# Combine weights by slot in one pass between gather products, and the last expert pair's weight splits moved back

## The chip, the cores and the metric

One core of a Trainium2 chip. The metric is the device time of one execution in microseconds (us); the kernel before takes 785.08 us, the median of three runs.

## The reference

`x` (256 tokens of 1024 features) passes a first block of two layers (sliding-window attention and a gated recurrence) and then a second block, whose last part is the one that matters here: a hierarchical mixture of experts and a gated projection.

```
g_val, g_idx = top_k(softmax(ht @ w_rg + b_rg), 1)          # one of 4 groups
e_val, e_idx = top_k(softmax(e_logits of that group), 2)     # two of its 4 experts
combine = sum(one_hot(g_idx * 4 + e_idx) * gate)             # tokens x 16
a, u = ht @ w_gate[e], ht @ w_up[e]                          # 1024 -> 256
hid = silu(a) * u * combine
x = x + sum over e of hid @ w_down[e]                        # 256 -> 1024
h3 = rms_norm(x, ple_norm_g)
x = x + sigmoid(h3 @ w_pg) * (p @ w_ple)
```

## The kernel before

Everything is in fp32. For the dense matrices a weight `w` is split into `whi` (a cast on ScalarE, ACT; L287) and `wlo = raw - whi` (on VectorE, DVE; L288), and three fp32r matmuls (L380 to L382) stand for one; the `raw` they are split from is streamed from `w_all` by SyncE (SP). The experts' weights are streamed by the same queue (L231), but used unsplit.

The expert stage goes as follows. Routing gives each token a place among the 64 slots of each of its two experts, and `D` (L1347; `slots[t]`, for `t` the first and second 128 tokens) is the 128 x 1024 matrix of ones and zeros that says which token stands in which slot; `NP` = 8 pairs of experts have 128 slots each. `gather(i, k, t, j)` (L1409) multiplies by `D` to bring the hidden rows (`hh`, `hl`) into slots, 512 slots at a time (`i` = 0, 1), for each of the eight blocks `k` of features; the four products over `t` and `j` sum up in one PSUM tile, copied to `hs`. `gate_up(q, j)` (L1460) multiplies the slots of pair `q` by half (`j`) of its gate and up weights. `product` forms the gated product `hid` on ACT (L1468) and DVE (L1469), where `cs` (the combine weight of each slot) comes in. `turn` transposes it to `hidT` (L1475, L1477), `down` gives `y` (L1488), split into `yh` and `yl` (L555), and `scatter` (L1503) brings it back to the tokens through `DT`, the transpose of `D` (`turn_slots`, L1430).

`to_slots` holds what needs doing once: counts of tokens by expert (`psp`, L1436, to `cnt` and `cnti`), `cs` from `psc` (L1442: for each pair `q` the product of `D` with the two columns of `comb` that belong to it, over both `t`), and `turn_slots(1)`. If any expert has more than 64 tokens, `overflow` (L1546) does the rest after a branch on `cnti`; otherwise each engine jumps over it. SP has its part in that branch.

The order on each engine is set by the Tile scheduler from the code's order, from `ahead` (a priority) and from `issue_after`. Weights are requested by `Stream.give`, a list of buffer kinds (`t4`: two transfers of 512 KB; `raw` and `t8`: one of 1 MB), and by `refill`, which gives again what a step has used up; a transfer waits on SP until its buffer's last reader is done, and those behind it on SP wait too. Once the last expert's weights are requested, `refill` goes on to the final projection's (`pg`) and prepares up to `cap` of its splits ahead, behind `st.after(*last)`, the split of `y` of the pair at hand; `cap` is set in `down` for the last three pairs:

```
        if q > NP - 4:
            g.st.after(*last)
            g.st.cap = (2, 4, 6)[q - NP + 3]
        g.st.refill()
```

Then `ple_out` does the rest: the last scatter and the addition to `x` (`finish`, L1512), `xw = x * wb` (L1612), transposes (`tr`, L1615), the split into `h3h` and `h3l`, and the products by `pg` (L380 to L382).

Of the kernel before, what the change touches and what calls it, by code (L numbers as in the profile page):

```python
# [9 lines left out]
F32 = mybir.dt.float32  # L10
F32R = mybir.dt.float32r
I32 = mybir.dt.int32
AF = mybir.ActivationFunctionType
OP = mybir.AluOpType
AX = mybir.AxisListType
# [10 lines left out]
NE = NG * EG  # L26
NP = NE // 2
# [581 lines left out]
def load_row(g, tag, src, n=DM):  # L609
    t = g.p.tile([128, n], F32, tag=tag, name=tag, bufs=g.nwb if tag == "wb" else 1)  # L610
    g.nc.sync.dma_start(out=t, in_=bcast(src))
    return t
# [630 lines left out]
def moe(g, last):  # L1243

    nc, h, p, fl, tc = g.nc, g.h, g.p, g.fl, g.tc
    g.nwb = 1
    wb = load_row(g, "wb", h["ffn_norm_g_2"][0])
# [10 lines left out]
    ps = g.sm.tile([128, 2, 256], F32, tag="s", name="pTp")  # L1258
# [21 lines left out]
    def small(name, shape, dt=F32):  # L1280
        return p.tile([128] + list(shape), dt, name=name)
# [4 lines left out]
    hh, hl, xw, rs, D = [], [], [], [], []  # L1286
    h2T = t8(g, "h2T")
    psr = g.sm.tile([128, 2, 20], F32, tag="s", name="psr")
    psp = g.sm.tile([128, 3, NE], F32, tag="s", name="psp")
    lg, oh, gd = (small(n, s) for n, s in (("lg", (2, 20)), ("oh", (2, 4)), ("gd", (2, 4))))  # L1290
    gm, kg, gsum, comb = small("gm", (2,)), small("kg", (2, 4)), small("gsum", (2,)), small("comb", (2, 4, 4))
    rank, sel, place = small("rank", (2, 4, 4)), small("sel", (2, 4, 4)), small("place", (2, NE))
    for t in range(2):
        xw.append(t4(g, f"xw{t}", shape=(128, DM)))
# [3 lines left out]
    flat = lambda a: a.rearrange("p g e -> p (g e)")  # L1298
# [51 lines left out]
    def combine(t):  # L1350

        le = lg[:, t, 4:20].rearrange("p (g e) -> p g e", e=4)
        m4, d, s4, ge = small(f"m4{t}", (4,)), small(f"d{t}", (4, 4)), small(f"s4{t}", (4,)), small(f"ge{t}", (4,))
        ex = lambda a: a.unsqueeze(2).to_broadcast([128, 4, 4])
        nc.scalar.activation(ge, gd[:, t], AF.Exp, accum_out=gsum[:, t:t + 1])
        nc.vector.tensor_reduce(m4, le, op=OP.max, axis=AX.X)
        nc.vector.tensor_sub(d, le, ex(m4))
        nc.scalar.activation(d, d, AF.Exp)
        nc.vector.scalar_tensor_tensor(d, rank[:, t], 2.0, d, op0=OP.is_lt, op1=OP.mult)
        nc.vector.tensor_reduce(s4, d, op=OP.add, axis=AX.X)  # L1360
        nc.vector.tensor_scalar(s4, s4, gsum[:, t:t + 1], None, op0=OP.mult)
        nc.vector.reciprocal(s4, s4)
        nc.vector.tensor_mul(s4, s4, oh[:, t])
        nc.vector.tensor_mul(comb[:, t], d, ex(s4))

    mr = []
    nc.tensor.matmul(psr.rearrange("p t c -> p (t c)"), g.c("ident"), g.c("zeros", 40), start=True, stop=True)

    def begin(t, b):
        if b == 0:  # L1370
            mr.append(MeanRoot(g, g.x[t], hh[t]))
        mr[t].half(b)
        return route(t, b)

    def end(t, moved):
        rs.append(mr[t].end())
        with tc.issue_after(moved.ins):
            for c in range(2):
                c2 = slice(c * 512, c * 512 + 512)
                nc.scalar.activation(hh[t][:, c2], xw[t][:, c2], AF.Copy, scale=rs[t])  # L1380
        choose(t)
        combine(t)

    with ahead(g, -20):
        begin(0, 0)
        begin(1, 0)
        moved = begin(0, 1)
        fl.fill(2)
        end(0, moved)
        fl.until(last)  # L1390
        fl.add(ple_job())
        g.st.prepare(g.st.limit)
        g.st.give("t4", "t4", "raw", "t4", "t4", "raw", "t4", "t4", "t8")
        end(1, begin(1, 1))
    fl.all()
    g.st.give("t8", "t4", "t4", "raw", "t4")
    cnt = small("cnt", (1,))
    cnti = small("cnti", (1,), I32)


    hs = [[t8(g, f"hs{i}", F32, (128, 4, 512)) for _ in range(2)] for i in range(2)]
    slots = [d.rearrange("p e s -> p (e s)") for d in D]
    held = {}

    def gather(i, k, t, j):
        ks = slice(k * 128, (k + 1) * 128)
        if t == 0 and j == 0:
            held[k] = g.acc.tile([128, 512], F32, tag="acc", name="acc")
        nc.tensor.matmul(held[k], (hh, hl)[j][t][:, ks], slots[t][:, i * 512:(i + 1) * 512],  # L1409
                         start=(t == 0 and j == 0), stop=(t == 1 and j == 1))  # L1410
        if t and j:
            copy = nc.vector.tensor_copy if k % 2 else nc.scalar.copy
            copy(hs[i][k // 4][:, k % 4], held[k])

    for t, j in ((0, 0), (0, 1), (1, 0), (1, 1)):
        for k in range(4):
            gather(0, k, t, j)
    for k in range(4, KT):
        for t, j in ((0, 0), (0, 1), (1, 0), (1, 1)):
            gather(0, k, t, j)  # L1420

    cs = small("cs", (NP,))
    DT = small("DT", (NP, 256), F32R)

    def turn_slots(t):
        for b in range(2):
            ps = g.sm.tile([128, 4, 128], F32, tag="s", name="DTp")
            for q in range(4):
                o = (4 * b + q) * 128
                nc.tensor.transpose(ps[:, q], slots[t][:, o:o + 128].bitcast(F32), g.c("ident"))  # L1430
            nc.scalar.copy(DT[:, 4 * b:4 * b + 4, t * 128:(t + 1) * 128], ps)

    def to_slots():

        for t in range(2):
            nc.tensor.matmul(psp[:, 2], g.c("ones"), flat(sel[:, t]), start=(t == 0), stop=(t == 1))  # L1436
        nc.vector.tensor_reduce(cnt, psp[:, 2], op=OP.max, axis=AX.X)
        nc.vector.tensor_copy(cnti, cnt)
        psc = g.sm.tile([128, NP, 2], F32, tag="s", name="psc")
        for q in range(NP):  # L1440
            for t in range(2):
                nc.tensor.matmul(psc[:, q], slots[t][:, q * 128:(q + 1) * 128].bitcast(F32),  # L1442
                                 flat(comb[:, t])[:, 2 * q:2 * q + 2], start=(t == 0), stop=(t == 1))
        for i in range(2):
            r = slice(64 * i, 64 * i + 64)
            nc.vector.tensor_copy(cs[r], psc[r, :, i])
        turn_slots(1)


    acc, hid, y = [], {}, {}  # L1450

    def gate_up(q, j):
        if j == 0:
            hid[q] = g.sm.tile([128, 512], F32, tag="s", name="au")
        w = [g.st.plain("gu", 512) for _ in range(2)]
        for k in range(4):
            kk = 4 * j + k
            for i in range(2):
                half, o = divmod(2 * q + i, 8)
                last = nc.tensor.matmul(hid[q][64 * i:64 * i + 64], hs[half][kk // 4][:, kk % 4, o * 64:(o + 1) * 64],  # L1460
                                 w[i][k // 2][:, k % 2], start=(kk == 0), stop=(kk == KT - 1), skip_group_check=True)
        g.st.refill()
        return last

    def product(q):
        ps = hid[q]
        a = p.tile([128, 256], F32, tag="hid", name="hid", bufs=2)
        nc.scalar.activation(a, ps[:, 0:256], AF.Silu)  # L1468
        nc.vector.scalar_tensor_tensor(a, a, cs[:, q:q + 1], ps[:, 256:512], op0=OP.mult, op1=OP.mult)  # L1469
        hid[q] = a  # L1470
# [8 lines left out]
    def down(q):  # L1479
        hT = hid.pop(q)  # L1480
        w = [g.st.plain("down", 1024) for _ in range(2)]
        y[q] = t4(g, "yh", F32R, (128, DM)), t4(g, "yl", F32R, (128, DM))
        for c in range(2):
            c2 = slice(c * 512, (c + 1) * 512)
            ps = g.sm.tile([128, 512], F32, tag="s", name="y")
            for k in range(2):
                for i in range(2):
                    nc.tensor.matmul(ps[64 * i:64 * i + 64], hT[:, k, 64 * i:64 * i + 64], w[i][k][:, 0, c2],  # L1488
                                     start=(k == 0), stop=(k == 1), skip_group_check=True)
            last = split_to(g, y[q][0][:, c2], y[q][1][:, c2], ps)  # L1490
        if q > NP - 4:
            g.st.after(*last)
            g.st.cap = (2, 4, 6)[q - NP + 3]
        g.st.refill()

    def scatter(q, t, cs=(0, 1)):
# [3 lines left out]
        for c in cs:  # L1500
            c2 = slice(c * 512, (c + 1) * 512)
            for i in range(2):
                nc.tensor.matmul(acc[t][c], DT[:, q, ts], y[q][i][:, c2],  # L1503
                                 start=(q == 0 and i == 0), stop=(q == NP - 1 and i == 1))
# [7 lines left out]
        nc.vector.tensor_add(g.x[t][:, c2], g.x[t][:, c2], acc[t][c])  # L1512

    tc.mark_branch_hint_location("past", "LikelyTaken", engines=list(ENGINES))
    turn_slots(0)
    with tc.issue_after(gate_up(0, 0).ins):
        to_slots()
    for k in range(KT):
        for t, j in ((0, 0), (0, 1), (1, 0), (1, 1)):
            gather(1, k, t, j)  # L1520
    gate_up(0, 1)
    product(0)
    overflow(g, cnti, wb, rs, place, comb)
    g.st.give("t4", "t4")
    g.wb = load_row(g, "wb", h["ple_norm_g_2"][0])
    for q in range(NP):
        if q + 1 < NP:
# [149 lines left out]
```

## Time and profile before

| | |
|---|---|
| median of 3 runs | 785.08 us (783.78 to 786.03) |
| the profiled execution | 785.89 us |
| its span | 784.1 us |
| TensorE (PE) busy | 757.3 us, 97% of the span |
| VectorE (DVE) busy | 451.9 us, 58% |
| ScalarE (ACT) busy | 350.3 us, 45% |
| DMA | 153.31 MB, mean 196 GB/s |
| chain that ended last | DMA `wx` 7%, DMA `raw` 5% of the span |

Busy is the time in which an engine has an instruction in execution; a matmul's record includes time in the pipeline, so that records overlap, and the step from one start to the next is the price of one. "Idle before" in brackets is the pause of that engine ahead of the row, with the instruction that ended it. The granted clock is the share of TensorE's 2.4 GHz that was given (0.50 is 1.2 GHz). Times count from the start of the span.

### The profile page before, as it was taken

To read this page: it belongs to the slowest core of one execution; us is meant where nothing else is said; L and a number is where in the kernel's file an instruction comes from. 1 tells how busy PE (TensorE), PEld (TensorE's weight loads), DVE (VectorE), ACT (ScalarE), POOL (GpSimd) and SP (SyncE) were. 2 spreads that over 40 slices of the span, in tenths; PEclk is the share of its full clock that TensorE was granted. 3 is DMA by queue.
4 is the path that set the end of the run, shared out by engine and by line. 5 is a ranking of instruction groups with operands and counts; after the bars stand their busy time and mean duration, and the time that the engine had idled before them with its cause. 6 is when DMAs were issued, how large, how long until landed. Compare 5 with 4: busy or idle time off the path is not lost. (4 is left out here: it accounts for less than half of the span.)

```text
span 784.1 us, 11957 instructions
## 1 busy us (share of the span) xinstructions
PE 757.3 (97%) x4894; PEld 620.4 (79%) x4894; DVE 451.9 (58%) x733; ACT 350.3 (45%) x581; POOL 21.8 (3%) x33
## 2 busy tenths in 40 slices
PE   8999999999999999999999999999999989999687
PEld 5899899899889989989988989999987743333256
DVE  6686477848677638777677767764645211111363
ACT  6761345744466115665555674663524121101241
POOL 0000000000000001000001300000000000000000
PEclk9999999999999999999999999999999899999889
DMA  8872134455257204427642632764479339999601
GB/s 300 323 273 101 31 132 162 159 217 215 109 208 261 94 1 138 143 84 295 241 150 81 227 124 82 260 226 155 158 266 384 129 120 404 418 416 417 263 1 54
DMA packets 29883, 153.31 MB, mean 196 GB/s; under 512 B 4600, under 2 KB 5632, under 8 KB 16768
## 3 DMA queue, kind: packets, MB, share of 16 engines
q1 hardware_dynamic: 29680, 152.45, 52.2%
q8 instruction: 39, 0.64, 0.3%
q14 instruction: 20, 0.16, 0.1%
q10 hardware_dynamic: 144, 0.07, 0.0%
HBM read 151.45 MB, written 1.05 MB: 194 GB/s over the span
## 5 line engine op out<-in xcount | busy, mean ns | idle before, releaser
L288 DVE TENSOR_TENSOR wlo<-raw,whi 128x1024 fp32r<-128x1024 f32 (+1 forms) x182 | 215.8, 1220 | 74.8 <-ACT whi L287 71.5
L287 ACT CAST whi<-raw 128x1024 fp32r<-128x1024 f32 (+1 forms) x182 | 182.4, 1050 | 35.5 <-DMA raw<-in_w_all_dram 34.3
L380 PE MATMUL acc<-hTh,whi 128*128 128x256 f32 x608 | 173.6, 285 | 0.0
L381 PE MATMUL acc<-hTl,whi 128*128 128x256 f32 x608 | 172.1, 283 | 0.0
L382 PE MATMUL acc<-hTh,wlo 128*128 128x256 f32 x608 | 171.9, 283 | 0.0
L382 PEld LDWEIGHTS acc<-hTh,wlo 128*128 128x128 f32 x608 | 114.7, 189 | 3.2 <-issue 3.2
L380 PEld LDWEIGHTS acc<-hTh,whi 128*128 128x128 f32 x608 | 114.5, 188 | 1.7 <-issue 1.2
L381 PEld LDWEIGHTS acc<-hTl,whi 128*128 128x128 f32 x608 | 114.6, 189 | 0.3 <-issue 0.2
L380 PE MATMUL acc<-whi,hTh 128*128 128x512 f32 (+2 forms) x224 | 84.9, 379 | 0.7 <-ACT whi L287 0.7
L381 PE MATMUL acc<-wlo,hTh 128*128 128x512 f32 (+2 forms) x224 | 84.1, 376 | 0.4 <-DVE wlo L288 0.4
L382 PE MATMUL acc<-whi,hTl 128*128 128x512 f32 (+2 forms) x224 | 83.8, 374 | 0.0
L1460 PE MATMUL au<-wx,hs 128*64 128x512 f32 x208 | 58.3, 597 | 0.0
L380 PEld LDWEIGHTS acc<-whi,hTh 128*128 128x128 f32 x224 | 42.2, 189 | 7.1 <-ACT whi L287 1.1
L381 PEld LDWEIGHTS acc<-wlo,hTh 128*128 128x128 f32 x224 | 42.3, 189 | 6.6 <-DVE wlo L288 0.7
L382 PEld LDWEIGHTS acc<-whi,hTl 128*128 128x128 f32 x224 | 42.2, 189 | 6.2
L1469 DVE SCALAR_TENSOR_TENSOR hid<-hid,cs,au 128x256 f32<-128x256 f32 x8 | 3.8, 480 | 69.2 <-ACT hid L1468 69.2
L380 PE MATMUL acc<-whi,mTh 128*128 128x512 f32 x96 | 38.5, 401 | 0.0
L381 PE MATMUL acc<-wlo,mTh 128*128 128x512 f32 x96 | 38.0, 396 | 0.0
L382 PE MATMUL acc<-whi,mTl 128*128 128x512 f32 x96 | 38.0, 396 | 0.0
L1460 PEld LDWEIGHTS au<-wx,hs 128*64 128x64 f32 x208 | 16.9, 136 | 24.3 <-issue 22.9
L1488 PE MATMUL y<-wx,hidT 128*64 128x512 f32 x96 | 29.6, 596 | 0.0
L922 PEld LDWEIGHTS sc<-QA,FK 128*128 128x128 f32 x192 | 27.6, 191 | 1.8 <-DVE QA L928 0.5
(329 smaller groups left out, 1242.6 us busy)
## 6 DMA issues: line engine op xcount, KB each, us to landing
raw<-in_w_all_dram SPq DMA_DIRECT2D x98, 1024.0 KB, 5.0
wx<-in_w_all_dram SPq DMA_DIRECT2D x72, 512.0 KB, 10.8
raw<-in_w_all_dram SPq DMA_DIRECT2D x2, 1040.0 KB, 4.8
wx<-in_w_all_dram SPq DMA_DIRECT2D x2, 1024.0 KB, 6.8
x<-in_x_dram SPq DMA_DIRECT2D x2, 512.0 KB, 5.0
wb<-in_norm_w_dram SPq DMA_DIRECT2D x2, 512.0 KB, 6.1
raw<-in_w_all_dram SPq DMA_DIRECT2D x2, 512.0 KB, 8.3
out_dram<-sig SPq DMA_DIRECT2D x3, 256.0 KB, 2.0
```

The costliest lines, as they stand in the source:

```text
L287: a = g.nc.scalar.copy(hi[:, :w], raw)
L288: b = g.nc.vector.tensor_sub(lo[:, :w], raw, hi[:, :w].bitcast(F32))
L380: nc.tensor.matmul(out, ah, bh, start=first, stop=False)
L381: nc.tensor.matmul(out, ah, bl, start=False, stop=False)
L382: nc.tensor.matmul(out, al, bh, start=False, stop=last)
L922: nc.tensor.matmul(ps[:, 4 * t + a], K[:, a, ts], q2t[:, a], start=True, stop=True)
L1460: last = nc.tensor.matmul(hid[q][64 * i:64 * i + 64], hs[half][kk // 4][:, kk % 4, o * 64:(o + 1) * 64], w[i][k // 2][:, k % 2], start=(kk ...
L1469: nc.vector.scalar_tensor_tensor(a, a, cs[:, q:q + 1], ps[:, 256:512], op0=OP.mult, op1=OP.mult)
L1488: nc.tensor.matmul(ps[64 * i:64 * i + 64], hT[:, k, 64 * i:64 * i + 64], w[i][k][:, 0, c2], start=(k == 0), stop=(k == 1), skip_group_chec ...
```

## The change

The combine weights `comb` are split into a high and a low fp32r part on DVE (`combs`), so that `psc` takes one matmul with four columns for each pair and `t`, where an fp32 matmul with two columns stood, and two reductions add the parts into `cs`. Those matmuls are written behind each block `k` of `gather(1)`. `turn_slots` takes one half of `D`'s slots at a time and is written behind blocks 4 to 7 of `gather(0)`, for both `t`. The counts come right after the routing. Of the two `t4` given behind the branch one is given before it, and `product(0)` is written behind it. `cap` goes from (2, 4, 6) to (0, 3, 6).

```diff
@@ moe, routing
+    combs = small("combs", (2, NE, 2), F32R)
...
         nc.vector.tensor_mul(comb[:, t], d, ex(s4))
+        hi, lo = (combs[:, t, :, i] for i in range(2))
+        nc.vector.tensor_copy(hi, flat(comb[:, t]))
+        nc.vector.tensor_sub(lo, flat(comb[:, t]), hi.bitcast(F32))
...
+    for t in range(2):
+        nc.tensor.matmul(psp[:, 2], g.c("ones"), flat(sel[:, t]), start=(t == 0), stop=(t == 1))
     fl.all()
     g.st.give("t8", "t4", "t4", "raw", "t4")
...
+    nc.vector.tensor_reduce(cnt, psp[:, 2], op=OP.max, axis=AX.X)
+    nc.vector.tensor_copy(cnti, cnt)
...
+    def turn_slots(t, b):
...
     for k in range(4, KT):
         for t, j in ((0, 0), (0, 1), (1, 0), (1, 1)):
             gather(0, k, t, j)
...
-        turn_slots(1)
+        turn_slots(k // 2 - 2, k % 2)
...
-            g.st.cap = (2, 4, 6)[q - NP + 3]
+            g.st.cap = (0, 3, 6)[q - NP + 3]
...
-    turn_slots(0)
-    with tc.issue_after(gate_up(0, 0).ins):
-        to_slots()
+    gate_up(0, 0)
+    psc = g.sm.tile([128, NP, 4], F32, tag="s", name="psc")
     for k in range(KT):
         for t, j in ((0, 0), (0, 1), (1, 0), (1, 1)):
             gather(1, k, t, j)
+        for t in range(2):
+            nc.tensor.matmul(psc[:, k], slots[t][:, k * 128:(k + 1) * 128], combs[:, t, 2 * k:2 * k + 2],
+                             start=(t == 0), stop=(t == 1))
+    for i in range(2):
+        r = slice(64 * i, 64 * i + 64)
+        nc.vector.tensor_reduce(cs[r], psc[r, :, 2 * i:2 * i + 2], op=OP.add, axis=AX.X)
+    g.st.give("t4")
     gate_up(0, 1)
+    overflow(g, cnti, wb, rs, place, comb)
+    g.st.give("t4")
     product(0)
-    overflow(g, cnti, wb, rs, place, comb)
-    g.st.give("t4", "t4")
```

What the scheduler makes of it, at the places that count. PE from the end of `gate_up(0, 0)` (`au`) on, before (the two rows of `psc` come eight times in all):

```order
L1460 MATMUL au<-wx_6118,hs_6136 64x512
L1436 MATMUL psp<-sel,const 128x16 x2
L1442 MATMUL psc<-comb,D_5891 128x2
L1442 MATMUL psc<-comb,D_5895 128x2
...
L1430 MATMUL DTp<-const,D_5895 128x128 x8
L1409 MATMUL acc<-D_5891,hh_5889 128x512
L1409 MATMUL acc<-D_5891,hl_5890 128x512
L1409 MATMUL acc<-D_5895,hh_5893 128x512
```

and of the change, from the end of the first gather on (the six rows of a block of `gather(1)` come eight times):

```order
L1417 MATMUL acc<-D_5896,hl_5895 128x512
L1431 MATMUL DTp<-const,D_5896 128x128 x4
L1453 MATMUL au<-wx_6033,hs_6145 64x512
...
L1453 MATMUL au<-wx_6125,hs_6145 64x512
L1417 MATMUL acc<-D_5892,hh_5890 128x512
L1417 MATMUL acc<-D_5892,hl_5891 128x512
L1417 MATMUL acc<-D_5896,hh_5894 128x512
L1417 MATMUL acc<-D_5896,hl_5895 128x512
L1513 MATMUL psc<-combs,D_5892 128x4
L1513 MATMUL psc<-combs,D_5896 128x4
```

The counts are gone from here (they stand ahead of `gather(0)`), the transposes stand ahead of `gate_up(0, 0)`, four of the second half's eight inside `gather(0)`, and `psc` is spread over `gather(1)`. The rows of a listed matmul on unsplit fp32 operands are two records in the trace.

SP from the last transfers ahead of the branch on (`wx` are the expert weights, one row 512 KB; `cnti` the count that the branch reads), before:

```order
L231 DMA wx_6307<-in_w_all_dram 128x1024
L231 DMA wx_6308<-in_w_all_dram 128x1024
L231 DMA wx_6311<-in_w_all_dram 128x1024
L231 DMA wx_6312<-in_w_all_dram 128x1024
L1545 TENSOR_LOAD cnti_6135
```

and of the change:

```order
L231 DMA wx_6304<-in_w_all_dram 128x1024
L231 DMA wx_6305<-in_w_all_dram 128x1024
L231 DMA wx_6316<-in_w_all_dram 128x1024
L231 DMA wx_6317<-in_w_all_dram 128x1024
L231 DMA wx_6320<-in_w_all_dram 128x1024
L231 DMA wx_6321<-in_w_all_dram 128x1024
L1543 TENSOR_LOAD cnti_6142
```

Two transfers have moved from behind the branch to ahead of it; the first of each list is the one that leaves before the long wait.

ACT at the end of the expert stage (`yh` is the split of `y`, `whi` that of the final projection's weights, two for each `raw`), before:

```order
L1468 ACTIVATE hid<-au 128x256
L287 CAST whi<-raw 128x1024 x2
L555 CAST yh<-y 128x512 x2
L1477 COPY hidT<-hTp 128x256
L287 CAST whi<-raw 128x1024 x2
L555 CAST yh<-y 128x512 x2
L287 CAST whi<-raw 128x1024 x2
```

and of the change:

```order
L1460 ACTIVATE hid<-au 128x256
L555 CAST yh<-y 128x512 x2
L1469 COPY hidT<-hTp 128x256
L287 CAST whi<-raw 128x1024 x3
L555 CAST yh<-y 128x512 x2
L287 CAST whi<-raw 128x1024 x3
```

The two `yh` of pair 6 and the transpose for pair 7 now come ahead of all `whi`, and the next `yh` behind three of them.

## Rows read from the trace of the kernel before

**Rows 1.** PE's timeline, 618 to 640 (start us, us, engine, line, operation; pause before it).

```profile
618.68 0.62 PE L1436 MATMUL psp<-sel,const 128*128 128x16 f32 x4
619.15 5.20 PE L1442 MATMUL psc<-comb,D 128*128 128x2 f32 x32
624.22 1.95 PE L1430 MATMUL DTp<-const,D 128*128 128x128 f32 x8
625.82 0.78 PE L1409 MATMUL acc<-D,hh 128*128 128x512 f32 x1
...
628.03 0.39 PE L1409 MATMUL acc<-D,hl 128*128 128x512 f32 x1
...
634.37 3.65 PE L1460 MATMUL au<-wx,hs 128*64 128x512 f32 x16
640.02 0.61 PE L1460 MATMUL au<-raw,hs 128*64 128x512 f32 x1 [1.99 <-DVEq L1546]
```

**Rows 2.** Table of stretches: us, busy of PE, PEld, DVE, ACT, POOL, clock, DMA, GB/s.

```profile
619.10:621.10 2.00, 2.00 (x20) 2.00 (x19) 0.17 (x1) 0.00 (x0) 0.00 (x0) 1.00 0.00 0
621.10:624.20 3.10, 3.10 (x16) 3.10 (x17) 0.00 (x0) 0.00 (x0) 0.00 (x0) 0.50 0.00 0
...
627.70:634.40 6.70, 6.70 (x31) 5.20 (x29) 2.07 (x3) 2.60 (x5) 0.00 (x0) 0.98 0.00 0
```

**Rows 3.** What SP waits for: in total us, times, longest.

```profile
SPq L231 <- PE acc L1409: 24.5, 2, 24.2
...
SPq L1546 <- SPq L1546: 6.6, 4, 2.7
```

**Rows 4.** Tile wx, transfers issued in 633 to 636 (issue durations in ns).

```profile
L231 SPq DMA_DIRECT2D wx<-in_w_all_dram x3: 328/383/422, 633.8 to 634.6; - x3
...
DMA to landing us min/median/max: 4.8/5.9/8.1
```

**Rows 5.** Table of stretches, the expert stage (columns as above).

```profile
646.00:735.00 89.00, 83.61 (x375) 31.10 (x371) 12.72 (x21) 13.57 (x29) 0.00 (x0) 0.99 0.99 403
```

**Rows 6.** PE's timeline, two successive pairs.

```profile
706.47 0.44 PE L1475 MATMUL hTp<-const,hid 128*128 128x128 f32 x2
...
719.50 0.44 PE L1475 MATMUL hTp<-const,hid 128*128 128x128 f32 x2
```

**Rows 7.** Chain of waits, where it enters the tail (start us, us, what).

```profile
721.14 13.45 DMA raw<-in_w_all_dram
```

**Rows 8.** ACT's timeline in the tail.

```profile
732.37 1.99 ACT L287 CAST whi<-raw 128x1024 fp32r<-128x1024 f32 x2 [8.42 <-DMA raw<-in_w_all_dram]
734.27 1.07 ACT L555 CAST yh<-y 128x512 fp32r<-128x512 f32 x2
```

**Rows 9.** PE's timeline in the tail.

```profile
734.90 0.79 PE L1503 MATMUL acc<-yh,DT 128*128 128x512 f32 x1 [5.39 <-ACT yh L555]
...
753.13 1.94 PE L1615 MATMUL tr<-const,xw 128*128 128x128 f32 x8 [3.77 <-DVE xw L1612]
754.90 0.79 PE L380 MATMUL acc<-whi,h3h 128*128 128x512 f32 x1
```

**Rows 10.** PE's timeline, start of the first gather.

```profile
606.47 1.96 PE L1409 MATMUL acc<-D,hh 128*128 128x512 f32 x4 [0.42 <-ACT ple L1275]
```

**Rows 11.** DVE's timeline, the second half's routing.

```profile
603.82 0.24 DVE L1315 SCALAR_TENSOR_TENSOR lg<-psr,rs,br 128x20 f32<-128x20 f32 x1 [2.03 <-PE psr L1310]
```

**Rows 12.** DVE's timeline in the tail.

```profile
749.98 1.28 DVE L1512 TENSOR_TENSOR x<-x,acc 128x512 f32<-128x512 f32 x2
751.17 1.22 DVE L288 TENSOR_TENSOR wlo<-raw,whi 128x1024 fp32r<-128x1024 f32 x1
752.31 1.28 DVE L1612 TENSOR_TENSOR xw<-x,wb 128x512 f32<-128x512 f32 x2
```

**Rows 13.** Table of stretches, the final projection (columns as above).

```profile
753.10:757.60 4.50, 4.47 (x14) 3.68 (x15) 2.19 (x6) 3.34 (x8) 0.48 (x1) 0.50 0.01 2
757.60:779.60 22.00, 22.00 (x123) 18.86 (x121) 10.10 (x16) 5.59 (x11) 0.62 (x2) 1.00 0.11 42
```

More of the change, by code (lines that the diff above doesn't have):

```diff
@@ L1413, in gather @@
             copy(hs[i][k // 4][:, k % 4], held[k])
+    cs = small("cs", (NP,))
+    DT = small("DT", (NP, 256), F32R)
+    def turn_slots(t, b):
+        ps = g.sm.tile([128, 4, 128], F32, tag="s", name="DTp")
+        for q in range(4):
+            o = (4 * b + q) * 128
+            nc.tensor.transpose(ps[:, q], slots[t][:, o:o + 128].bitcast(F32), g.c("ident"))
+        nc.scalar.copy(DT[:, 4 * b:4 * b + 4, t * 128:(t + 1) * 128], ps)
     for t, j in ((0, 0), (0, 1), (1, 0), (1, 1)):
@@ L1420, in moe @@
             gather(0, k, t, j)
[L1422 to L1446, printed above, removed]
-        turn_slots(1)
+        turn_slots(k // 2 - 2, k % 2)
     acc, hid, y = [], {}, {}
@@ L1459, in gate_up @@
                 half, o = divmod(2 * q + i, 8)
-                last = nc.tensor.matmul(hid[q][64 * i:64 * i + 64], hs[half][kk // 4][:, kk % 4, o * 64:(o + 1) * 64],
+                nc.tensor.matmul(hid[q][64 * i:64 * i + 64], hs[half][kk // 4][:, kk % 4, o * 64:(o + 1) * 64],
                                  w[i][k // 2][:, k % 2], start=(kk == 0), stop=(kk == KT - 1), skip_group_check=True)
         g.st.refill()
-        return last
     def product(q):
```

## The prediction

> **What bounds the kernel now.** I read three things in this order: the timeline of TensorE (PE) around the expert stage with the table of stretches beside it, then what SyncE (SP, which issues the weight transfers) waits for, then the chain of waits through the end of the expert stage.
>
> The timeline first. Between `gate_up(0,0)` and `gather(1)` PE does 7.1 us of small work: token counts at 618.68, the combine weights by slot (`psc`) from 619.15 to 624.22, and `turn_slots(1)` to 625.82 [rows 1]. The table of stretches shows that the clock fell meanwhile: 18 of the `psc` records take 2.0 us at a granted clock of 1.00, the other 16 take 3.1 us at 0.50, that is 1.2 GHz, and it is back only inside `gather(1)` [rows 2].
>
> Behind that, the transfers. SP stands 24.2 us at one wait on a `gather` matmul [rows 3], so nothing is issued until 633.8; then three transfers leave, and SP waits 6.6 us in all at the branch of L1546, up to 2.7 at once [rows 3], until they have landed, the last 8.1 us after its issue at 634.6 [rows 4]. From 646 to 735 the DMA engines are busy 0.99 of the time at 403 GB/s [rows 5]. A pair of experts needs 6.29 MB (two experts, three 1024 x 256 matrices of 4 bytes), at 403 GB/s 15.6 us, but PE takes only 13.0 us a pair (706.47 to 719.50) [rows 6]. So the head start of the weights shrinks by some 2.6 us with each pair, and what the stream brings last is late.
>
> Last are the weights of the final projection (`raw`, then `whi` on ScalarE (ACT) and `wlo` on VectorE (DVE)). The chain of waits enters the tail through the second `raw`, 721.14 + 13.45 = 734.59 [rows 7]. ACT has the splits of the first `raw` ahead of `yh(6)` in its queue: it idles 8.42 us for that transfer and reaches `yh` at 734.27 [rows 8], and PE, in order, idles 5.39 us for `yh` with all of `y(7)` behind it [rows 9]. **So two things end the expert stage: when the stream starts, and that pair 6's output stands behind a transfer.** From the first product of the final projection at 754.90 [rows 9] to the end at 784.1 it is 29.2 us of mostly full-clock PE work.
>
> **The change, part by part.**
>
> *PE up to the end of `gather(1)`.* Gone from the stretch: counts 0.47, `psc` 5.07, `turn_slots(1)` 1.60 (differences of starts [rows 1]), and the half clock in `gather(1)`: 625.82 to 628.03 for five matmuls, 2.21 us, against 0.231 each at full clock (628.03 to 634.37 is 27 of them in 6.34, of which 0.10 is the step to the next kind), so 1.05. Together 8.2. Added: eight transposes in `gather(0)`, 1.6 us for eight at half clock [rows 1], half of that if the clock is all that matters; I take 1.0; and 16 `psc` products. They now have four columns and fp32r operands, so one record each instead of two. The price of one is not in the trace; the nearest row is the two-column record at full clock, 2.0 / 18 = 0.111 us [rows 2]. The bounds are 0.05 (half, if the weight load hides under the wide product before it) and 0.22 (what it costs at half clock). I take 0.111 plus 0.09 for each of the eight changes back to a wide product (an estimate from the 0.10 of that step between kinds): 1.8 + 0.7 = 2.5. Net 8.2 − 3.5 = **4.7 us earlier**; by the cheapest and dearest of these prices 6.6 and 2.4.
>
> A rule by itself: the Trainium skill (TensorE: Matmul & The Clock Gate, section LDWEIGHTS) gives a weight load as its columns over 1.2, 107 ns for 128 columns. By it the sixteen cost 1.7 instead of 1.8 us, and a load hidden under the previous product would save most of that.
>
> *What has cover.* The counts' two matmuls stand in the 0.42 us that PE waits for `ple` before `gather(0)` [rows 10]. The four DVE operations that split `comb` are of the size of that stage's others, 0.24 [rows 11]: those of the first half lie in DVE's 2.03 us idle stretch before 603.82 [rows 11]; those of the second, with the two of the counts, push `hl` and the last `D` of `gather(0)` by up to four times that. The rows show no idle of PE there, nor how near it is: I take 0, and 1.0 as the other bound. The two reductions for `cs` end before `hid` is ready at 638: 0.
>
> *The branch.* Before it PE loses 1.99 us to DVE's branch [rows 1]. The words of the change put the first `product` behind it, but in the built order ACT's and DVE's `hid` of pair 0 still stand ahead of the load of `cnti`, as before. I cost this at 0; the other bound is −1.99.
>
> *The stream.* SP's first issue behind `gather(1)` moves from 633.8 to 629.1. One transfer of four stood ahead of the wait before and one of six does now: five leave behind it, not three. The three took 9.0 us from the first issue to the last landing [rows 4]; two more at 0.524 MB / 403 GB/s = 1.3 us each [rows 5] make 11.6, so SP is released at 640.7 (639.5 if part of the third's 8.1 us was a delay of its own and not the rate), against 642.8. And these two need not be loaded afterwards: 2.6 us less. The stream is earlier by 2.1 + 2.6 = 4.7 to 3.3 + 2.6 = 5.9; I take **5.3**. PE does not run into its weights: the last expert piece is ahead of the first `raw` in the queue, so it landed about 2.6 us before 732.37, and PE's shift of 4.7 is less than the stream's.
>
> A rule that speaks here, by itself: the Trainium skill (DMA: Bandwidth & Descriptors, Where 436 GB/s comes from) says that reads from HBM are held to about 358 GB/s a core. The trace differs, with 403 over 89 us; by the page a transfer is 1.46 us and the two are worth 2.9, not 2.6.
>
> *The tail.* ACT now has `yh(6)`, `hidT`, then three splits, `yh(7)`, three splits. With 5.3 off: first `raw` at 727.1, second at 729.3. `y(7)` no longer waits for either. `whi` 0 and 1 (1.99 for two [rows 8]) to 729.1, `whi` 2 729.3 to 730.3, `yh(7)` (1.07 for two) to 731.4. DVE: `wlo` 2 to 731.5, `yl(7)` (1.28 for two) to 732.8, the last scatter to about 733.5; the four additions to `x` (1.28 for two [rows 12]) overlap it and end at 735.7; three `wlo` at 1.14 to 1.22 [rows 12] end at 739.2. There `xw` starts; it started at 752.31 [rows 12]. **Gain 13.1**, of which 5.3 is the stream and 7.8 the tail's order. The third `raw` is issued when the first buffer is free, about 730.3, and lands some 5 later (the first of three alone took 4.8 [rows 4]), in time for its splits.
>
> From `xw` on nothing changes: 2.59 to the first product. PE rests longer before it, and already today it begins at half clock (753.1 to 757.6 at 0.50 after 3.77 us without a matmul [rows 9, 13]), so I charge nothing.
>
> The profiled execution took 785.89 for a span of 784.1; the median is 785.08, 0.8 below. I subtract 13.0 from the median: **772.1 us**. With PE's part between 2.4 and 6.6 the stream, which starts with it, gains between 2.4 and 7.8, so 774.9 to 769.5; with the tail's serial parts 1 us to either side the forecast's own range is 768.5 to 776.
>
> **Rivals.**
>
> *The tail gives nothing.* If the third split (which needs the second `raw`) holds `yh(7)` as the first two held `yh(6)`, the additions and three splits in a row on DVE eat what the order gains. For it: `yh(7)` does stand behind a transfer, and DVE's tail has as many operations as before. Against: before, all of `y(7)` stood behind that wait; now only its scatter does. Then only the stream's 5.3 counts: 779.8. Chance 0.10.
>
> *The clock falls inside `gather(1)`.* It fell while PE ran narrow products without a pause [rows 2], and 16 of those now lie between the wide ones. At half clock 32 wide products cost 0.2 more each (0.43 against 0.231), 6.4 us: 778.5. For: the row. Against: `psc` is now a fifth of the stretch, not all of it. Chance 0.06.
>
> *It does at the branch what it says.* If `hid` is no longer waited for there, 1.99 less on PE, but the stream sets the end, so 0 to 2: 770 to 772. Chance 0.05.
>
> *Slower.* PE now rests longer before the final projection, some 8 us (733.5 to 741.8) instead of 3.77. The Trainium skill (TensorE: Matmul & The Clock Gate, HAM oscillation) says that idle gaps bring the clock to half and the work after them starts slow; the trace agrees, with 4.5 us at 0.50, and that much is in today's time already. The rival is that it stays low: the 22.0 us at full clock from 757.6 to 779.6 [rows 13] would cost up to 22 more, 794. It decides, against my 13, once more than 13 us of that work runs at half clock. For: the stretch does start at half clock. Against: it came back after 4.5 us there, and inside `gather(1)` too [rows 2, 13]. Chance 0.03.
>
> *Both gains vanish* (SP drains as late as before, and the first rival): within 0.3% of before. Chance 0.02.
>
> **How the numbers follow.** The forecast has 0.74. A difference under 0.3%, 2.4 us, is about what a measurement of this kernel cannot tell from no change. The forecast and the three rivals below 780 are all faster by more than that: with something off for the unforeseen, faster 0.93, same 0.03, slower 0.04. The range goes from 768.0 to 779.5: most of the forecast's 0.74, the clock and branch rivals, and half of the first.
>
> **What would show it.** `psc` sixteen records of about 0.11 within `gather(1)`, whose granted clock stays at 1.00; `gather(1)` ending at 629 to 630; five transfers leaving there and SP released at 639 to 641; still 2 us lost at the branch; the first `raw` landing about 727; no idle of ACT before `yh(6)`; `y(7)` done before 730; `xw` at 739. I am wrong if the first product of the final projection comes after 746, if its clock is low beyond some 5 us, or if the stream is ahead by under 4 us.

## The result, and the profile after

| | before | after |
|---|---|---|
| median | 784.73 us (783.78 to 786.03, 4 runs) | **774.49 us** (774.1 to 777.13, 4 runs) |
| after / before | | 0.9876, 95% interval 0.9849 to 0.9902 |
| profiled execution, its span | 785.89, 784.1 us | 777.13, 775.3 us |

The change gains 10.2 us; the forecast was 13.0 (772.1 us). The profiled execution of after is the longest of its four (the others have 774.1 to 774.6), so the two profiles stand for 8.8 us of gain (784.1 to 775.3); a second profile of the same code, `after_again` below, is read beside it.

First PE around the expert stage after the change (start, us busy, engine, line, operation, out<-in, size, count; idle time before and what ended it in brackets). These rows answer to [rows 1].

```profile
608.84 1.73 PE L1417 MATMUL acc<-D,hl 128*128 128x512 f32 x4
610.36 1.93 PE L1417 MATMUL acc<-D,hh 128*128 128x512 f32 x4
...
618.02 3.65 PE L1453 MATMUL au<-wx,hs 128*64 128x512 f32 x16
...
622.63 0.28 PE L1513 MATMUL psc<-combs,D 128*128 128x4 f32 x2
...
623.78 0.28 PE L1513 MATMUL psc<-combs,D 128*128 128x4 f32 x2
```

`gather(1)` follows `gate_up(0,0)` at once. A block with its two `psc` takes 1.15 us (622.63 to 623.78); four wide products at 0.231 are 0.93, so two `psc` cost 0.22, eight times that 1.8. The table of stretches (as [rows 2]) has the clock:

```profile
609.00:611.00 2.00, 2.00 (x6) 1.39 (x6) 2.00 (x4) 0.00 (x0) 0.00 (x0) 0.51 0.99 397
621.60:630.90 9.30, 9.30 (x52) 7.92 (x50) 2.11 (x4) 2.93 (x5) 0.00 (x0) 1.00 0.01 2
740.00:745.00 5.00, 0.68 (x4) 0.71 (x5) 4.78 (x6) 0.21 (x1) 0.00 (x0) 0.72 0.09 36
745.00:750.00 5.00, 5.00 (x17) 3.99 (x17) 2.91 (x6) 4.19 (x8) 0.55 (x1) 0.60 0.00 2
```

In `gather(1)` it is 1.00 throughout, where it had been 0.50 [rows 2]. But in `gather(0)` it is now 0.51: four wide products take 1.52 us (608.84 to 610.36), 0.38 each. That stretch had no such fall in the profile before.

Then the branch, again PE:

```profile
630.87 3.65 PE L1453 MATMUL au<-wx,hs 128*64 128x512 f32 x16
636.49 0.61 PE L1453 MATMUL au<-raw,hs 128*64 128x512 f32 x1 [1.97 <-DVEq L1544]
...
639.41 0.64 PE L1453 MATMUL au<-raw,hs 128*64 128x512 f32 x1 [0.98 <-issue]
```

The 1.97 us for DVE's branch stayed. New is a pause of 0.98 three us later. The profile shows no releaser for it, and by the trace the weights that this row multiplies had landed by 614.6, long before; what PE waits for there stays open. How long the transfers that leave from 630 on took to land (four of the five have a figure: in order 4.6, 5.8, 8.1 and 8.9), and what SP waited for (engine, line, releaser; us in total, times, longest):

```profile
DMA to landing us min/median/max: 4.6/6.9/8.9
```

```profile
SPq L231 <- PE acc L1417: 19.1, 1, 19.1
SPq L1544 <- SPq L1544: 8.0, 6, 2.8
```

SP's long wait shrank from 24.2 to 19.1, its wait in the branch grew from 6.6 to 8.0 [rows 3]. The first issue is at 630.16 (633.8 before), and SP goes on some 11.5 later.

Now the end of the expert stage, PE, ACT and DVE (as [rows 9], [rows 8], [rows 12]):

```profile
727.63 0.44 PE L1467 MATMUL hTp<-const,hid 128*128 128x128 f32 x2
729.03 1.07 PE L1480 MATMUL y<-raw,hidT 128*64 128x512 f32 x2
...
735.27 1.07 PE L1480 MATMUL y<-wx,hidT 128*64 128x512 f32 x2
744.32 1.94 PE L1613 MATMUL tr<-const,xw 128*128 128x128 f32 x8 [5.84 <-DVE xw L1610]
```

```profile
729.53 1.99 ACT L287 CAST whi<-raw 128x1024 fp32r<-128x1024 f32 x2 [0.93 <-DMA raw<-in_w_all_dram]
731.96 1.05 ACT L287 CAST whi<-raw 128x1024 fp32r<-128x1024 f32 x1 [0.44 <-DMA raw<-in_w_all_dram]
...
736.38 0.59 ACT L555 CAST yh<-y 128x512 fp32r<-128x512 f32 x1 [2.89 <-PE y L1480]
```

```profile
740.09 3.49 DVE L288 TENSOR_TENSOR wlo<-raw,whi 128x1024 fp32r<-128x1024 f32 x3
743.49 1.28 DVE L1610 TENSOR_TENSOR xw<-x,wb 128x512 f32<-128x512 f32 x2
```

ACT no longer idles 8.42 us for a `raw` [rows 8]; its longest wait there, 2.89, is for PE's `y(7)`. `y(7)` began at 729.03 and ended only at 736.3. The chain of waits, the pieces of the end:

```profile
724.11 3.58 PE y L1480 x16
...
729.10 1.00 PE y L1480 x2
730.11 0.43 PE acc L1495
730.54 1.86 PE y L1480 x6
732.40 0.42 PE acc L1495
732.82 1.86 PE y L1480 x6
734.68 0.66 PE acc L1495 x2
735.34 1.02 PE y L1480 x2
736.38 0.59 ACT yh L555
...
740.17 3.40 DVE wlo L288 x3
743.57 0.61 DVE xw L1610
```

Before, the largest shares of the chain were the transfers of `wx` and `raw`, and it entered the tail by a `raw` [rows 7]. Now no transfer is among its pieces from 610 on: **the expert stage ends on PE**, then on the queue of DVE. From `xw` on nothing changed: 784.1 − 752.31 [rows 12] and 775.3 − 743.49 are both 31.8 us.

### The profile page after: what moved, and what is told of

It is laid out like the page before. It is cut to its first block, busy times and chain, and to the rows that moved or that the text cites. A ratio compares the mean times of both kernels' runs of the same rounds, so it can differ in the third digit from the quotient of the medians.

```text
span 775.3 us, 11929 instructions
## 1 busy us (share of the span) xinstructions
PE 752.3 (97%) x4878; PEld 617.8 (80%) x4878; DVE 452.8 (58%) x737; ACT 350.2 (45%) x581; POOL 21.8 (3%) x33
## 3 DMA queue, kind: packets, MB, share of 16 engines
HBM read 151.45 MB, written 1.05 MB: 197 GB/s over the span
```

## The experiments

Two theories of the result stood against each other. One (theory A below): after the change PE ends the stage, so that time is won only by work of PE up to pair 7 and by the order of the tail. The rival (theory B), which the prediction's sum used: the weight stream still ends it. Ratios are to runs of the kernel before on the same chip, with their 95% interval. "hTp(7)" is the start of pair 7's transposes on PE; the tail is the span from there to the end. The kernel before has

```profile
729.07 0.44 PE L1475 MATMUL hTp<-const,hid 128*128 128x128 f32 x2
```

so its tail is 784.1 − 729.07 = 55.0 us; after has 775.3 − 727.63 = 47.7.

**caps_only**: the kernel before, with the later splits alone.

```
-            g.st.cap = (2, 4, 6)[q - NP + 3]
+            g.st.cap = (0, 3, 6)[q - NP + 3]
```

> The kernel before with nothing but the last pairs' limits on prepared splits at (0, 3, 6). Theory A, the tail hangs on when TensorE reaches the last pair: from its hidden transpose (hTp, 729.1 before) to the start of xw it takes 15.9 us as in the changed kernel instead of 23.2, so xw at 744.9 and 777.4 us (a gain of 7.4). Theory B, the tail hangs on the raw transfers alone, as the prediction worked it out: with raw unmoved xw at 744.5, 777. Both say that the limits alone give most of the whole gain. Rival C, the new order pays only with an earlier stream: no gain, 783 to 785.

Measured: 779.18 us (777.39 to 779.65), ratio 0.9914 [0.9895, 0.9933]: 5.9 us of the gain, some 2 us less than both theories said. In the profile the tail is 48.4 us, and `xw` (745.29) starts 15.9 us behind hTp(7), as theory A has it. PE with the 32 old `psc`, and three stretches:

```profile
621.02 3.71 PE L1442 MATMUL psc<-comb,D 128*128 128x2 f32 x32
```

```profile
608.00:612.00 4.00, 4.00 (x11) 2.94 (x11) 2.32 (x4) 0.24 (x1) 0.00 (x0) 0.62 1.00 387
621.00:624.60 3.60, 3.60 (x35) 3.60 (x34) 0.17 (x1) 0.00 (x0) 0.00 (x0) 1.00 0.00 0
...
639.50:642.80 3.30, 3.30 (x11) 1.09 (x9) 0.00 (x0) 0.00 (x0) 0.00 (x0) 0.53 0.08 17
```

The same 32 narrow products, back to back, ran at a clock of 1.00, and the half clock stood in two other places: in `gather(0)` and behind the branch. So the half clock of [rows 2] does not belong to `psc`.

**gather_only**: the changed kernel with the old caps, so the other half of the change.

```
-            g.st.cap = (0, 3, 6)[q - NP + 3]
+            g.st.cap = (2, 4, 6)[q - NP + 3]
```

> The changed kernel with the limits put back to (2, 4, 6). The tail then hangs on the raw transfers again, and the gain is their shift. Theory A (the shift seen in the profiled run of the change, 2.8 us, with up to 1.5 more where the clock does not fall in the first gather): 780.4 to 781.9. Theory B (the prediction's 5.3): 779.4. Rival: within 0.3% of before.

Measured: 782.11 us (781.82 to 783.19), ratio 0.9962 [0.9945, 0.9978]: 3.0 us, 0.2 beyond the slow end of theory A's range, where theory B had 779.4. The parts alone give 5.9 + 3.0 = 8.9, both together 9.6 to 10.2: they nearly add. hTp(7) is at 726.06, 3.0 earlier than before, and the tail has 54.0. ACT shows why it is still so long:

```profile
727.99 1.99 ACT L287 CAST whi<-raw 128x1024 fp32r<-128x1024 f32 x2 [7.05 <-DMA raw<-in_w_all_dram]
```

With the old caps `yh(6)` stands behind a transfer as in [rows 8]: 7.05 us of ACT's time are lost there, with the combine weights by slot already moved.

**after_again**: the changed kernel, unedited, on another chip.

> The changed kernel once more, unedited, on the chip of the next three. Theory A: the half clock that its first profile shows in the first gather (608 to 612, about 1 us) comes and goes with the execution, as the half clock in the weights by slot did before; a profile without it has a span of about 773 and PE reaches the last pair's transpose near 726 instead of 727.6. Rival: it belongs to the new order and is there again, at 608 to 612. The time: 774.5.

Measured: 776.23 us (775.85 to 776.62) beside 785.82 before, ratio 0.9883 [0.9863, 0.9902]. The stretch of `gather(0)` that had 0.51 in the first profile:

```profile
608.00:612.00 4.00, 3.68 (x15) 2.41 (x16) 3.40 (x14) 1.60 (x4) 0.00 (x0) 1.00 1.00 407
```

So the same code falls to half clock there in one execution and not in another. PE did not reach pair 7 near 726, though: its first transposes began 1.15 us later in this execution (605.82 against 604.67), and hTp(7) is at 727.60. The branch is as in the first profile:

```profile
636.62 0.61 PE L1453 MATMUL au<-raw,hs 128*64 128x512 f32 x1 [1.97 <-DVEq L1544]
...
639.38 0.64 PE L1453 MATMUL au<-raw,hs 128*64 128x512 f32 x1 [0.82 <-issue]
```

**psc_block**: all sixteen `psc` in one block ahead of `gather(1)`.

```
     for k in range(KT):
-        for t, j in ((0, 0), (0, 1), (1, 0), (1, 1)):
-            gather(1, k, t, j)
         for t in range(2):
             nc.tensor.matmul(psc[:, k], ...
+    for k in range(KT):
+        for t, j in ((0, 0), (0, 1), (1, 0), (1, 1)):
+            gather(1, k, t, j)
```

> The changed kernel with the sixteen weight products in one block ahead of the second gather instead of two behind each feature block. Theory A: what counts is sixteen records in place of thirty-two, spreading them is worth nothing: 0.11 us each, 1.8 in all, the time of the change within 0.3%. Rival: in a block they bring the clock down as the thirty-two did, which costs 1 to 3 us: 775.5 to 777.5.

Measured: 776.72 us (775.16 to 777.14), ratio 0.9885 [0.9863, 0.9908], no different from after_again. The time fits both sides of the expectation; the trace decides between them (the clock over the block is 1.00):

```profile
620.10 1.95 PE L1511 MATMUL psc<-combs,D 128*128 128x4 f32 x16
621.91 0.48 PE L1417 MATMUL acc<-D,hh 128*128 128x512 f32 x1
```

Sixteen take 1.81 us in a block (starts 620.10 to 621.91) and 1.8 spread. What saved time is one record instead of two, not the spreading.

**hid_behind**: `product(0)` really behind the branch; the block that is jumped over also writes its tile, and `hid[0]` lies in another PSUM pool.

```
+    a0 = p.tile([128, 256], F32, tag="hid", name="hid", bufs=2)
-    overflow(g, cnti, wb, rs, place, comb)
+    overflow(g, cnti, wb, rs, place, comb, a0)
...
-    product(0)
+    product(0, a0)
```

> The changed kernel with the first gated product really behind the branch (its tile is also written inside the overflow block, and its sums lie in the other PSUM pool). Theory A: the 1.97 us that TensorE waits at the branch cover a wait for the third of the five transfers (it lands 9.0 us after the first is issued and ends a further 0.98); without the first the second grows to some 2.9, and the time is that of the change within 0.3%. Rival, the prediction's: 0 to 2 us less.

Measured: 775.37 us (774.95 to 779.65), ratio 0.9871 [0.9852, 0.989]: no different. PE:

```profile
635.06 0.61 PE L1454 MATMUL au<-raw,hs 128*64 128x512 f32 x1 [0.44 <-PEq L1547]
...
639.75 1.01 PE L1454 MATMUL au<-raw,hs 128*64 128x512 f32 x1 [2.36 <-issue]
```

The wait at the branch falls from 1.97 to 0.44, and the second pause grows from 0.98 to 2.36 (in a profile that is the longest of its five runs) and ends at about the same time (639.75 against 639.41). So the branch wait is worth nothing alone. That the second pause is a wait for the third transfer, as the expectation has it, is not shown: in the kernel before PE runs through the same rows from 641.76 on without a pause, and its third transfer lands only at 642.8.

**gives_behind**: both `t4` given behind the branch again, so three transfers ahead of it.

```
-    g.st.give("t4")
     overflow(g, cnti, wb, rs, place, comb)
-    g.st.give("t4")
+    g.st.give("t4", "t4")
```

> The changed kernel with both requests behind the branch again, so that three transfers leave ahead of it and not five. Theory A: what SP is released earlier (2.5 us) it has to load later, so the stream stays where it is, and the third transfer lands 9.0 us after the first issue in both: no change, 776.2 within 0.3%. Rival: the move was worth its 2.5 us of transfers, 778.5.

Measured: 774.79 us (773.99 to 776.53), ratio 0.9867 [0.9848, 0.9887]: no different. SP goes on at 638.5 instead of 642.1, and the two transfers that the change had moved ahead have to be issued then; PE sees no gain either way.

**after_nowb** and **gather_nowb**: the transfer of the last norm's weights (L611) left out, in the changed kernel and in gather_only.

```
-    g.wb = load_row(g, "wb", h["ple_norm_g_2"][0])
+    g.wb = wb
```

> The changed kernel without the transfer of the last norm's weights (512 KB behind the branch; the last norm uses those of the norm before instead, which changes the output). All that follows in the stream comes 1.3 us earlier, nothing else moves. Theory A, the tail hangs on TensorE's arrival at the last pair and on its products there: no change, within 0.3% of the changed kernel (776.2 on this scale). Theory B, the tail hangs on the stream as the prediction worked it out: 1.3 us less.

> The same transfer left out, and the last norm scaled as before it, in the changed kernel with the limits put back to (2, 4, 6). There the first splits stand ahead of the last but one pair's output, so both theories tie the tail to the first raw: 1.3 us less than that kernel, which took 782.1 (0.9962 of the kernel before): 0.9945.

Measured: 775.85 us (775.04 to 776.66), ratio 0.9881 [0.9862, 0.9899], against 0.9883 for the unedited kernel: nothing. And 780.97 us (776.85 to 781.95), ratio 0.9947 [0.9926, 0.9968] against gather_only's 0.9962 [0.9945, 0.9978]: 1.2 us less, but the intervals overlap. In the first the stream did come earlier, the split of the first `raw` at 728.65 instead of 729.53, and `xw` stayed (743.37 and 743.49): 0.9 us off the stream buys nothing after the change. The second is inconclusive by its times, but its profile, which is its fastest run (776.85), shows something else. PE in the tail, the stretch 728 to 734, first gather_only, then gather_nowb:

```profile
728.00:734.00 6.00, 2.71 (x5) 1.41 (x6) 4.93 (x6) 5.12 (x7) 0.00 (x0) 0.66 0.30 93
```

```profile
728.00:734.00 6.00, 4.32 (x14) 1.48 (x14) 5.00 (x6) 3.23 (x6) 0.00 (x0) 1.00 0.53 176
```

With the first `raw` split 1.9 us earlier (726.10 against 727.99) PE pauses 0.94 instead of 4.02 us for `yh`, its clock stays at 1.00, and from its first scatter to `xw` it takes 15.55 instead of 17.62. So with the old caps the tail does hang on the first `raw`, and behind the long pause some 2 us of it are half clock, by this one execution. The kernel before has the same, behind its 5.39 us [rows 9]:

```profile
734.90:740.60 5.70, 4.93 (x7) 1.69 (x7) 4.37 (x5) 2.60 (x4) 0.00 (x0) 0.50 0.58 191
```

**caps033**: three of the last six splits left until after `xw`.

```
-            g.st.cap = (0, 3, 6)[q - NP + 3]
+            g.st.cap = (0, 3, 3)[q - NP + 3]
```

> The changed kernel with limits (0, 3, 3): three splits less stand on VectorE between the additions to x and xw, the rest come behind the split of h3. Theory A, after the last addition VectorE's queue is the bound: xw starts 3.4 us earlier, 771.1 us. Rival: the later splits now hold the final projection's products, and the gain is given back: 773 to 776.

Measured: 771.07 us (769.97 to 771.17), ratio 0.9814 [0.9798, 0.9831]. The tail is 42.1 us, 5.6 shorter than after's. DVE, then PE:

```profile
737.09 1.36 DVE L1504 TENSOR_TENSOR x<-x,acc 128x512 f32<-128x512 f32 x2
738.37 1.29 DVE L1610 TENSOR_TENSOR xw<-x,wb 128x512 f32<-128x512 f32 x2
```

```profile
739.20 1.17 PE L1613 MATMUL tr<-const,xw 128*128 128x128 f32 x8 [1.24 <-DVE xw L1610]
```

The three `wlo` (3.49 us) ahead of `xw` are gone, and `xw` now also comes ahead of the other half's additions: 738.37 − 727.11 = 11.3 behind hTp(7), where after has 743.49 − 727.63 = 15.9. PE rests 1.24 instead of 5.84 us and starts the final projection at a clock of 1.00. From the start of `tr` to the end it takes 30.0 us (31.0 after), although three splits are made there that after had made before.

**early_branch**: the branch moved from behind `gather(1)` to right behind `gate_up(0,0)`.

```
-    g.st.give("t8", "t4", "t4", "raw", "t4")
+    g.st.give("t8", "t4", "raw")
...
     gate_up(0, 0)
+    overflow(g, cnti, wb, rs, place, comb)
+    g.st.give("t4", "t4")
...
-    overflow(g, cnti, wb, rs, place, comb)
```

(`hid[0]` in the other PSUM pool, as in hid_behind.)

> The changed kernel with the overflow branch directly behind gate_up(0,0) (the sum tile of pair 0 in the other PSUM pool, two of the weight requests moved behind the branch). SP then passes the branch with nothing in flight. Theory A, in the change TensorE loses 1.97 us at the branch and 0.98 to a weight transfer behind it, and both come from where the branch stands: 3 us less, 771.5. Rival: the weights requested behind the branch come late for pair 1 and TensorE waits for them instead: 774 to 777.

Measured: 774.08 us (773.9 to 774.25), ratio 0.9857 [0.9841, 0.9874]. Both pauses of PE behind `gather(1)` are gone, which gains 3.2 us by hTp(0) (7.0 us behind the start of `gate_up(0,1)` instead of 10.25 in after_again). But `gate_up(0,0)`, now ahead of the branch, takes 4.77 us (616.57 to 621.34) instead of 3.58. So hTp(7) stands at 724.31, 120.1 us behind the start of the first transposes of `D` (604.24); that is 121.8 in after_again and 123.0 in after. Its interval overlaps after_again's, so the 0.8 to 1.4 us by which it is ahead of the unedited kernel (11.0 against 10.2 and 9.6) rest on the trace more than on the times. It misses the 771.5 of theory A; it lies at the edge of the rival's 774 to 777, but the trace shows no wait of PE for weights of pair 1.

**early_033**: early_branch with caps (0, 3, 3); **early_022**: the same with (0, 2, 2).

> The early branch and the limits (0, 3, 3) together. Theory A: the first takes about 1.5 us off TensorE's way to the last pair, the second 3.4 off VectorE's queue behind it, one after the other: 769.6. Rival: with TensorE earlier, the splits that now come later hold the final projection: 771 or more.

> The early branch with limits (0, 2, 2): only the splits of the first raw stand ahead of pair 7's output. Theory A: the third split costs nothing ahead of that output, since TensorE ends the products of pair 7 later than it; the time is that of (0, 3, 3), 768.1, or up to 1 us worse where the final projection waits for its second half kilobyte of weights. Rival: pair 7's output comes earlier by the split's 1.0 us: 767.1.

Measured: **768.09 us** (768.0 to 769.11) beside 785.82, ratio 0.9784 [0.9764, 0.9804], the fastest version found: 17.7 us less than before and 8.1 less than the changed kernel beside it. And 770.16 us (770.1 to 770.41), ratio 0.9813 [0.9796, 0.983], so (0, 2, 2) is not better, and worse than both sides of its expectation. In early_033 SP is through its part of the branch at 609, where after had it stand there until 641.7 (queue instructions of that line: count, ns, first and last start):

```profile
L1546 SPq EVENT_SEMAPHORE  x8: 17/17/17, 608.5 to 609.1; - x8
```

and the clock stays up in the final projection:

```profile
736.00:745.00 9.00, 8.24 (x38) 6.32 (x39) 8.25 (x13) 7.72 (x12) 0.55 (x1) 1.00 0.00 1
```

In early_022 PE runs into splits that are not there yet, which accounts for 1.4 of the 2.3 us (0.0029 of 785.8) by which it is slower than early_033:

```profile
742.11 0.50 PE L380 MATMUL acc<-whi,h3h 128*128 128x512 f32 x1 [0.62 <-ACT whi L287]
743.37 0.51 PE L381 MATMUL acc<-wlo,h3h 128*128 128x512 f32 x1 [0.76 <-DVE wlo L288]
```

## Why the prediction was right, and where it was off

*What bounds the kernel before: right.* The two causes it named can be taken away one by one: the caps alone give 5.9 us, the work around `gather(1)` alone 3.0, and with the latter alone ACT still idles 7.05 us for a `raw`. The measured time lies near the forecast; that does not confirm the sum behind it, since three of its steps came out otherwise, as follows.

*PE up to the end of `gather(1)`: 4.7 forecast; 4.1 and 5.1 measured.* From the first transposes of `D` to `gate_up(0,1)` it took 30.3 us (604.09 to 634.37), now 26.2 (604.67 to 630.87), and 25.2 in after_again. The transposes cost 1.0 as forecast, the sixteen `psc` 1.8 where 2.5 was taken: the estimate of 0.09 for each change back to a wide product was too much. What cost the 1.0 between the two profiles is the half clock in `gather(0)`. That is also what was wrong in the reasoning here: 3.1 us of the stretch's cost (1.5 of `psc`, 0.6 of the transposes, 1.05 in `gather(1)`) was half clock, and it was credited as if it went with the narrow products. caps_only keeps those at full clock.

*What has cover, and the branch at 0: nearly right.* PE waits 0.28 us at most for a `D` (after_again), and the counts put the start of `gather(0)` off by 0.3 (2.69 us behind the first transposes of `D`, 2.38 before): 0.6 where 0 was taken, within the bound of 1.0. `hid` still stands ahead of the branch and PE still loses 1.97 there; hid_behind shows that making the change do what it says would be worth 0.

*PE's lead up to pair 7: 4.7 taken, 2.0 and 3.2 measured.* The sum carried PE's 4.7 unchanged from `gate_up(0,1)` to pair 7. "PE does not run into its weights" holds as far as the traces show: no row of PE there waits for a transfer. But PE gave back 1.2 us (1.0 in after_again) at the pause behind the branch, whose cause is open, and 0.9 in pair 3 (13.87 us instead of 13.0), which is no wait but the built order: two of its sixteen `y` products stand apart from the others, behind eight scatter products. Relative to the first transposes, hTp(7) is 2.0 us earlier than before in the first profile and 3.2 in after_again.

*The stream: its length right, its lead too large.* SP was released 11.5 us after the first issue (11.6 forecast), at 641.7. But the first issue moved by 3.6, not 4.7, and the first `raw` landed at 729.5, 2.8 earlier than before [rows 8] where 5.3 was taken (3.4 if counted from the first transposes). So two of the prediction's own signs of being wrong came true: the stream is ahead by less than 4 us, and the first product of the final projection comes at 746.08, after 746.

***The tail: the step that failed.*** "`y(7)` no longer waits for either" is true; but the sum let it be ready (before 730) and made the second `raw` and the splits set the times. The traces show that PE sets them: `y(7)` starts at 729.03 and, with the scatter of pair 6 in between, ends at 736.3, 8.7 us behind hTp(7) where the sum had room for at most 5.6 (724.4 to 730). So `yh(7)` begins its second half at 736.38 (the sum had it done at 731.4), and `xw` comes 15.9 us behind hTp(7). That distance is 15.9 (15.86 to 15.88) in all eight profiles with caps (0, 3, 6): after, after_again, caps_only, psc_block, hid_behind, gives_behind, after_nowb and early_branch. In these the split of the first `raw` starts between 0.9 us behind hTp(7) (hid_behind and early_branch, without any wait for it) and 1.9 (after_again), so the stream does not set it.

The sum for `xw`: it came at 743.49, 4.3 later than the 739.2 forecast. Had PE been at pair 7 at 729.07 − 4.7 = 724.4, it would have come at 740.2: 1.0 is the mis-sized work of PE behind hTp(7). 2.7 is PE's lead, 2.0 instead of 4.7, and 0.6 the later start of the first transposes in that execution (604.67 against 604.09). The tail's order, put at 7.8, gave 7.4 (23.24 us from hTp(7) to `xw` before, 15.86 now). That this is near is in part luck: some 2 us of the 23.24 were the half clock behind PE's long pause, by gather_nowb's profile, and the sum has no term for it. Had the sum been made on PE's queue, the tail would have been read as "hTp(7) plus PE's remaining work, then DVE's queue", and the next step, fewer splits ahead of `xw`, would have been in plain sight: caps033 takes 4.6 us off that distance.

*The rivals.* "The tail gives nothing" is false: 55.0 us became 47.7. The clock did not fall inside `gather(1)`. The slower rival, that the clock stays low in the final projection, is false as well: it is at 0.72 and 0.60 from 740 to 750, as it was at 0.50 for 4.5 us before [rows 13], and then full. What was left out is that the start at half clock can be avoided. The Trainium skill (TensorE: Matmul & The Clock Gate, HAM oscillation) says that idle gaps bring the clock to half and the work behind them starts slow. The trace agrees for the long pause (5.84 us, then 0.60); behind a pause of 1.24 in the same place the clock stayed at 1.00 (caps033 and early_033).

## What to carry to other kernels

When a wait is taken out of an engine's queue, redo the sum of the stage on the next thing in line, here TensorE's own work with its order, and don't leave the old releaser as the clock of the stage. Prices read at half clock in one profiled execution are not the price of the instructions that happened to run there; a second profile of the same code tells. In this kernel the branch on all engines cost less where no transfer was under way (early_branch; 1.7 us at hTp(7), 0.8 to 1.4 in the time), and splits for a later stage were cheapest where they lay neither ahead of the last results of this one (caps033) nor behind their first use (early_022).

## What the hardware showed unexpectedly

- **The half clock moves between executions.** The same `gather(0)` (608 to 612) had a granted clock of about 0.5 to 0.6 in the profiles of caps_only, after, caps033, hid_behind and after_nowb, and 1.00 in those of after_again, gather_only, psc_block, gives_behind, early_branch and three more. In after's `gather(0)` it cost 1.0 us against after_again, and in the profile of the kernel before it stood in another place [rows 2]. Nor does the length of a pause decide it alone: behind the two us at the branch the clock stayed at 1.00 in before, after and after_again and fell to 0.5 in caps_only and gives_behind. What sets it is open.
- **Transfers behind the idle queue land late.** Behind `gather(1)` the third took 8.1 us from its issue to its landing in the kernel before and 8.0 to 8.5 in five profiles after the change, with three under way or five, while the first took 4.8 and 4.6. Why the third is slower than the rate of [rows 5] would make it was not tried.
- **A pause of PE without a releaser.** In the profiles of the changed order that keep the branch behind `gather(1)`, PE stops some three us behind it for 0.5 to 1.2 us (2.36 in hid_behind), amid products whose operands are there. early_branch, with the branch elsewhere, does not have it there, and caps_only, with the old order, does not either. No run here shows what it waits for.
- **Column halves lose their overlap when other work lies between.** Two products with 64 columns each run at the same time: in after two start at 730.47, one by `raw` and one by `wx`, and the next two 0.48 later, where the two at 729.03, behind each other, take 1.01. Sixteen `y` records in a row take 3.58 us in the chain; `y(7)`, broken up by four scatter products (0.43, 0.42 and 0.66 for the last two), took 1.00 + 1.86 + 1.86 + 1.02 = 5.74.
